# Normalised rows turned by VectorE in 32x32 blocks and placed by a trip through DRAM, for the first six token tiles of LN1

## The chip, the cores and the metric

The kernel runs on one core of one Trainium2 chip. The metric is device time of one execution in microseconds (us). Of three runs of the kernel before, the median is 2017.85 us, the lowest 2013.26, the highest 2018.37. A separate execution was profiled; its trace gives the lines in this document.

The core has five engines with instruction queues of their own: TensorE (PE in the trace, with PEld for its weight loads), VectorE (DVE), ScalarE (ACT), GpSimd (POOL) and SyncE (SP). TensorE multiplies operands from SBUF into PSUM, the accumulator memory. VectorE and ScalarE read SBUF and PSUM. DMA transfers are issued here from the queues of SP and ACT.

## The reference

One layer of a bidirectional encoder, 1024 tokens by 1024 features, float32. Cut to what matters here:

```python
h = layer_norm(x, ln_in_g, ln_in_b)
proj = h @ w_in                                  # attention and recurrence inputs, gates
...
merged = sigmoid(ga) * (att @ w_att_up) + sigmoid(gh) * (rec @ w_hgrn_up)
h = layer_norm(alpha * h + merged @ w_o, ln1_g, ln1_b)
gate, up = split(h @ w_ffn_in)                   # 1024 x 5632
h = layer_norm(alpha * h + (silu(gate) * up) @ w_ffn_out, ln2_g, ln2_b)
```

`layer_norm` takes the mean and variance over the 1024 features of a token, normalises, and applies a gain and a shift per feature. The change lies between the first LN1 (the fifth line) and the product with `w_ffn_in`: the normalised rows have tokens on partitions, and the FFN product needs features on partitions.

## The kernel before

**Stages.** The kernel runs three phases one after the other on the same engines: LN of the input, the projection, attention and recurrence (phase 1); the two up-projections, the gates, W_o and LN1 (phase 2); the FFN and LN2 (phase 3). Each large product is split into three: a float32 operand is cast to a short form "hi" (ScalarE) and a remainder "lo" (GpSimd or VectorE, line 229), and `mm3` (lines 277 to 279) adds hi x hi, hi x lo and lo x hi. The FFN products go by a scheme of Winograd and Strassen kind: seven products of half size (`PRODUCTS`) on sums and differences of the operand's quarters. The quarters and sums of LN1's result are called b11, b21, b22, t1, t2, t3 and t4, and are kept as pairs in `self.xb`.

**The stage of the change** is the last loop of `phase2` (lines 1532 to 1577), over eight tiles `t` of 128 tokens. For each tile:

- `split` makes the hi and lo of the merged activations (`mh`, `ml`).
- `y` (two buffers) is loaded from `ahs_d` by SP: alpha times the residual (line 1545).
- `half(0)` and `half(1)` each multiply by one half of W_o: 24 matmuls of 128x512 into one of four PSUM banks ("pj"), which line 1554 adds to `y` on VectorE.
- `rest(t, y)` takes statistics (lines 206 to 215), normalises (`normalise`, line 300 on ScalarE; for tile 7 half of it on VectorE, line 1524), calls `h1_blocks`, and stores the normalised rows to `n1_d` from ACT's queue (line 1530).

`h1_blocks` turns the 128x1024 rows with `transposed` (lines 302 to 308): two groups of four TensorE transposes by the identity, each into a PSUM bank ("sd"). From the bank, gain and shift are applied per feature (line 1600 on ScalarE, line 1602 on VectorE). Tiles 0 to 3 give b11 and b21, and `w11` (line 1609). Tiles 4 to 7 give t1 (line 1626), b22, t2, t3 and t4; t1 and t2 are put in place at once, the others are stored to `td` in DRAM (line 1618) and read back by `ffn_again` (line 1737).

The order for tiles 0 and 1 is half(0) of both, half(1) of tile 0, `rest(0)`, half(1) of tile 1. After tile 7's halves the first two products (on b11 and b21) of the first three FFN column groups are written ahead of `rest(7)`.

**What sets the order.** The program is given to a planner that simulates all engines with estimated costs, and issues what is ready by priority, which is the order of the program; `high_priority` moves instructions ahead in that order. The result is a fixed list per engine and queue. On the chip each list runs in order, and an instruction that waits holds up those behind it in its list.

**Buffers.** Pool `ws` has a tag "wkeep" with three buffers of 128x512. In the FFN, `keep` (line 1680) copies partial products into them, the first three in the products written ahead of `rest(7)`. Before that the tag isn't used in this stage. A buffer is free when every reader of its tile is done.

Of the kernel before, what the change touches and what calls it, by code (L numbers as in the profile page):

```python
# [10 lines left out]
F32 = mybir.dt.float32  # L11
# [11 lines left out]
HALF = 512  # L23
# [56 lines left out]
class Block:  # L80
    evac_ahead = 1000

    def __init__(self, ctx, tc, x, ln_in_g, ln_in_b, w_in, hgrn_lb, hgrn_norm_g, w_att_up, w_hgrn_up,
                 w_o, ln1_g, ln1_b, w_ffn_in, w_ffn_out, ln2_g, ln2_b, tabs, out, dbg=None):
        self.tc, self.nc, self.ctx = tc, tc.nc, ctx
        self.x = x[0]
        self.ln = {"in": (ln_in_g, ln_in_b), "1": (ln1_g[0], ln1_b[0]), "2": (ln2_g[0], ln2_b[0])}
        self.w_in, self.lbw, self.ng = w_in[0], hgrn_lb, hgrn_norm_g[0]
        self.wa, self.wr, self.wo = w_att_up[0], w_hgrn_up[0], w_o[0]
        self.wfi, self.wfo, self.tabs, self.out = w_ffn_in[0], w_ffn_out[0], tabs, out[0]  # L90
        self.dbg = dbg or {}
        nc = self.nc

        self.npj = 0
        self.issued = {}
        self.psum = ctx.enter_context(tc.tile_pool(name="psum", bufs=1, space=PSUM))
        self.cst = ctx.enter_context(tc.tile_pool(name="cst", bufs=1))
        self.tiny = ctx.enter_context(tc.tile_pool(name="tiny", bufs=1))
        self.spare = self.pad(self.cst, CST_PAD)
        self.wpool = self.pool("wp", "right")  # L100
        self.wp = self.wpool.__enter__()
        dram = ctx.enter_context(tc.tile_pool(name="dram", bufs=1, space=DRAM))

        def scratch(name, n):
            if name in self.dbg:
                return [self.dbg[name][i] for i in range(n)]
            return [dram.tile([128, 1024], F32, name=f"{name}{i}") for i in range(n)]

        self.att_d = scratch("att", 4)
        self.rec_d = scratch("rec", 8)  # L110
        self.tg_d = scratch("tg", 16)
        self.n1_d = scratch("n1", 8)
        self.ahs_d = scratch("ahs", 8)
        self.hg_d = [{n: dram.tile([128, T], F32, name=f"hg{h}{n}") for n in ("t0", "t1", "q")}
                     for h in range(8)]
        self.at_d = [{(k, g): dram.tile([128, T], F32, name=f"at{j}{k}{g}") for k in "qk" for g in range(3)}
                     for j in range(4)]
        for h in range(8):
            self.hg_d[h].update({n: dram.tile([T, 128], F32, name=f"hg{h}{n}") for n in "vg"})
        for j in range(4):  # L120
            self.at_d[j].update({("v", g): dram.tile([T, 128], F32, name=f"at{j}v{g}") for g in range(3)})
        self.w_d = [dram.tile([32, 128], F32, name=f"wd{j}") for j in range(4)]
        self.td = [dram.tile([128, 4, HALF], F32, name=f"td{i}") for i in range(3)]
        self.gd = {p: dram.tile([128, NF // 2, HALF], F32, name=f"gd{p}") for p in range(1, 8)}
        self.consts()
# [1289 lines left out]
    def phase2(self):  # L1415
        nc = self.nc
        with ExitStack() as es:
# [27 lines left out]
            for d in range(8):  # L1445
                t = tgate(d)
# [27 lines left out]
            for d in range(8):  # L1474
                t = tgate(8 + d)
# [23 lines left out]
            for z in (rows, self.recp, self.stp):  # L1499
# [4 lines left out]
                       for n in ("t1", "b11", "b21", "t2")}  # L1504
            yp = es.enter_context(self.pool("yp"))
            w11 = [(yp if k < 3 else self.ws).tile([128, HALF], F32, name="w11", tag=f"w11{k}" if k < 3 else "wsum",
                                                   bufs=1 if k < 3 else 3) for k in range(4)]
            raws = []

            def follow():  # L1510
# [5 lines left out]
                self.again = {n: self.ffn_again(n, 384) for n in ("b22", "t3")}  # L1516
                self.spread("b22")

            def rest(t, y):

                with self.tc.high_priority(offset=2 * self.evac_ahead if t == 7 else 0):
                    mv = self.stats(yp, y, "1")
                    if t == 7:
                        nc.vector.tensor_scalar(y[:, 0:HALF], y[:, 0:HALF], mv[:, 0:1], mv[:, 2:3], op0=OP.subtract,
                                                op1=OP.mult)
                        self.normalise(yp, y[:, HALF:D], y[:, HALF:D], mv)
                    else:
                        self.normalise(yp, y, y, mv)
                    self.h1_blocks(yp, t, y, w11, last=t >= 3)
                nc.scalar.dma_start(self.n1_d[t], y)  # L1530

            for t in range(8):
                ms = []
                for k0 in (0, 4):
                    mh, ml = self.granules()
                    tk = slice(128 * (t % 4), 128 * (t % 4) + 128)
                    if t < 4:
                        for k in (0, 2):
                            self.split(mh[:, k:k + 2, :], ml[:, k:k + 2, :], m0[(k0 + k) // 2][:, :, tk],
                                       eng_lo="dve" if t == 0 and k0 else "pool")  # L1540
                    else:
                        self.split(mh, ml, m1[:, k0:k0 + 4, tk])
                    ms += [(mh[:, k, :], ml[:, k, :]) for k in range(4)]
                y = yp.tile([128, D], F32, name="y1", tag="y1", bufs=2)
                nc.sync.dma_start(y, self.ahs_d[t])

                def half(hh, y=y, ms=ms, t=t):
                    ps = self.ps_pj()
                    for k, (mh, ml) in enumerate(ms):
                        whi, wlo = (z[:, k, :] for z in wo[hh])  # L1550
                        self.mm3(ps, mh, ml, whi, wlo, k == 0, k == KT - 1)
                    s = slice(HALF * hh, HALF * (hh + 1))
                    with self.tc.high_priority(offset=self.evac_ahead if t == 7 else 0):
                        nc.vector.scalar_tensor_tensor(y[:, s], ps, 0.5, y[:, s], op0=OP.mult, op1=OP.add)

                half(0)
                if t == 0:
                    second = half, y
                    continue
                if t == 1:  # L1560
                    second[0](1)
                    rest(0, second[1])
                half(1)
                if t == 7:
                    follow()
                if t in (5, 6):
                    raws.append(self.ffn_raws(t - 5))
                if t == 6:
                    raws.append(self.ffn_raws(2, self.wraw, ("wraw0", "wraw1"), 1))
                if t == 7:  # L1570
                    self.first_groups = [self.wino_project(raws[f], lambda *a, f=f: self.first_evac[f](*a), 1 + f)
                                         for f in range(3)]
                    for g in self.first_groups:
                        next(g)
                rest(t, y)
                if t == 7:
                    self.spread("t3", self.t2_last)
# [2 lines left out]
    PRODUCTS = {5: ("s1", "t1"), 1: ("a11", "b11"), 2: ("a12", "b21"), 6: ("s2", "t2"), 3: ("s4", "b22"),  # L1580
                7: ("s3", "t3"), 4: ("a22", "t4")}

    def h1_blocks(self, pool, t, y, w11, last=False):

        nc = self.nc
        c = slice(128 * (t % 4), 128 * (t % 4) + 128)
        gc, bc = self.col["g1"], self.col["b1"]

        def put(name, v):
            hi, lo = self.xb[name]  # L1590
            return self.split(hi[:, :, c], lo[:, :, c], v,
                              eng_lo="dve" if last else "pool")

        def scaled(q, ps, on_act):

            v = pool.tile([128, 4, 128], F32, name="tsv", tag="tsv", bufs=2)
            for k in range(4):
                g, b = (z[:, 4 * q + k:4 * q + k + 1] for z in (gc, bc))
                if k in on_act:
                    nc.scalar.activation(v[:, k, :], ps[k], AF.Identity, bias=b, scale=g)  # L1600
                else:
                    nc.vector.tensor_scalar(v[:, k, :], ps[k], g, b, op0=OP.mult, op1=OP.add)
            return v

        if t < 4:
            ps = self.transposed(y, 0)
            v = scaled(0, ps, ())
            for k in range(4):
                nc.scalar.activation(w11[k][:, c], ps[k], AF.Copy, scale=gc[:, k:k + 1])
            put("b11", v)  # L1610
            put("b21", scaled(1, self.transposed(y, 1), (0, 2)))
            return

        def later(i, name, v):
# [6 lines left out]
            return pool.tile([128, 4, 128], F32, name="tsum", tag="tsum", bufs=3)  # L1621

        t1, t2 = tmp(), tmp()
        ps = self.transposed(y, 0)
        for k in range(4):
            ins = nc.vector.scalar_tensor_tensor(t1[:, k, :], ps[k], gc[:, k:k + 1], w11[k][:, c], op0=OP.mult,
                                                 op1=OP.subtract)
        b22 = scaled(1, self.transposed(y, 1), (0, 1, 2, 3) if t < 7 else (0, 2))
        put("t1", t1)
        nc.vector.tensor_sub(t2, b22, t1)  # L1630
        self.t2_last = put("t2", t2).ins.name
# [440 lines left out]
```

## Time and profile before

| | |
|---|---|
| median of three runs | 2017.85 us |
| the profiled execution's own time | 2016.71 us |
| its span, first to last instruction | 2014.9 us |
| granted TensorE clock (mean) | 0.997 |
| the stage's W_o matmuls | 1279.64 to 1372.93 us in the span |
| transposes of `h1_blocks` (line 306) | 64, from 1304.8 to 1385.4 us |

All other times in this document are us from the start of the span, unless ns is written. In rows of instructions, `out<-in` names the tiles written and read (buffer numbers left out), `xN` counts instructions, and a bracket at the end holds the idle time ahead of an instruction and what ended it. Matmuls overlap, so the distance between their starts, not their duration, is what each one costs. In rows of windows, the numbers are busy us of the engines, with counts. In rows of DMA issues, the last number is the median time in us from issue to landing.

### The profile page before, as it was taken

Reading aid. Unit: us, or ns where it says so; the run is one execution under the profiler, and the core shown is the slowest. Engines: PE = TensorE matmul, PEld = TensorE weight load, DVE = VectorE, ACT = ScalarE, POOL = GpSimd, SP = SyncE. Lnnn points to the kernel's source line nnn. Section 1 sums busy time; section 2 is a strip of 40 time slices with the busy share of each in tenths; the row PEclk is TensorE's granted clock in tenths of the full one; section 3 lists DMA queues with packets and bytes.
Section 4 is the critical chain, followed back from the end, with each engine's and each line's share of the span. In section 5 each row is a group of like instructions: output and inputs, shape, how many; then the busy total and the mean of one; then the engine's idle time right before and its main releaser. Section 6 shows DMA issues by size and latency. Waiting matters only on the chain. (4 is left out here: it accounts for less than half of the span.)

```text
span 2014.9 us, 30820 instructions
## 1 busy us (share of the span) xinstructions
PE 1980.5 (98%) x10718; PEld 1640.8 (81%) x10718; DVE 1364.5 (68%) x2217; ACT 907.1 (45%) x1822; POOL 1006.3 (50%) x874
## 2 busy tenths in 40 slices
PE   7999999999999999999999999999999999999998
PEld 6688888888888888888888888888788888888886
DVE  7877746885467855797443236558777776767788
ACT  6554455543654446444464443345333333344541
POOL 6466643666455654565546562244666665620000
PEclk9999999999999999999999999999999999999999
DMA  5445645546455464555546377534434443447533
GB/s 162 126 121 151 164 131 149 140 119 173 108 158 141 132 156 118 152 147 151 141 122 190 121 252 245 156 121 141 140 127 136 145 137 125 144 166 276 167 103 123
DMA packets 416125, 301.17 MB, mean 149 GB/s; under 512 B 133153, under 2 KB 359394, under 8 KB 415970
## 3 DMA queue, kind: packets, MB, share of 16 engines
q1 hardware_dynamic: 410624, 282.14, 47.9%
q10 hardware_dynamic: 5346, 17.08, 2.2%
q8 instruction: 84, 1.38, 0.3%
q14 instruction: 71, 0.58, 0.1%
HBM read 204.96 MB, written 94.18 MB: 148 GB/s over the span
## 5 line engine op out<-in xcount | busy, mean ns | idle before, releaser
L229 POOL TENSOR_TENSOR w_lo<-wa,w_hi 128x512 fp32r<-128x512 f32 x272 | 366.3, 1355 | 230.5 <-ACT w_hi L219 216.6
L219 ACT CAST w_hi<-wa 128x512 fp32r<-128x512 f32 x272 | 168.2, 620 | 263.7 <-PE pj L278 166.2
L229 POOL TENSOR_TENSOR w_lo<-wsum,w_hi 128x512 fp32r<-128x512 f32 x88 | 127.8, 1462 | 111.1 <-PE sd L279 60.7
L229 POOL TENSOR_TENSOR w_lo<-f_raw,w_hi 128x512 fp32r<-128x512 f32 x66 | 101.2, 1540 | 51.5 <-ACT w_hi L219 50.3
L215 POOL TENSOR_TENSOR mv<-mv,mhalf 128x1 f32<-128x1 f32 x16 | 12.6, 790 | 221.7 <-DVE mv L214 221.6
L219 ACT CAST w_hi<-wsum 128x512 fp32r<-128x512 f32 x88 | 54.6, 621 | 116.7 <-PE sd L278 108.8
L277 PE MATMUL pj<-xt1hi,w_hi 128*128 128x512 f32 x252 | 99.0, 393 | 0.7 <-DVE evh L589 0.7
L219 ACT CAST gwsum<-a_raw 128x512 fp32r<-128x512 f32 (+1 forms) x78 | 48.1, 617 | 112.2 <-PE pj L278 56.0
L278 PE MATMUL pj<-xt1lo,w_hi 128*128 128x512 f32 x252 | 98.5, 391 | 0.0
L279 PE MATMUL pj<-xt1hi,w_lo 128*128 128x512 f32 x252 | 98.2, 390 | 0.0
L607 DVE TENSOR_TENSOR evh<-wkeep,pj 128x512 f32<-128x512 f32 x45 | 30.8, 685 | 99.4 <-PE pj L279 58.1
L727 POOL TENSOR_TENSOR wa<-wa,wa 128x512 f32<-128x512 f32 x46 | 65.8, 1431 | 57.1 <-DVE wa L726 56.2
L229 POOL TENSOR_TENSOR w_lo<-ws,w_hi 128x512 fp32r<-128x512 f32 x46 | 62.9, 1374 | 56.3 <-ACT w_hi L219 45.8
L755 ACT COPY wkeep<-pj 128x512 f32<-128x512 f32 x136 | 79.4, 585 | 4.9 <-DVE evh L577 4.7
L277 PE MATMUL pj<-xt2hi,w_hi 128*128 128x512 f32 x192 | 77.2, 403 | 2.0 <-ACT w_hi L219 2.0
L279 PE MATMUL pj<-xt2hi,w_lo 128*128 128x512 f32 x192 | 76.3, 397 | 2.0 <-POOL w_lo L229 2.0
L229 DVE TENSOR_TENSOR gwkeep<-a_raw,gwsum 128x512 fp32r<-128x512 f32 (+1 forms) x78 | 53.1, 681 | 36.1 <-ACT gwsum L219 33.3
L278 PE MATMUL pj<-xt2lo,w_hi 128*128 128x512 f32 x192 | 76.1, 396 | 0.8 <-DVE xt2lo L409 0.7
L277 PE MATMUL pj<-xt4hi,w_hi 128*128 128x512 f32 x192 | 76.2, 397 | 0.0
L278 PE MATMUL pj<-xb11lo,w_hi 128*128 128x512 f32 x192 | 75.3, 393 | 0.0
L278 PE MATMUL pj<-xt4lo,w_hi 128*128 128x512 f32 x192 | 75.2, 392 | 0.0
L277 PE MATMUL pj<-xb11hi,w_hi 128*128 128x512 f32 x192 | 75.0, 393 | 0.1
(438 smaller groups left out, 6481.7 us busy)
## 6 DMA issues: line engine op xcount, KB each, us to landing
wa<-in_w_in_dram SPq DMA_DIRECT2D x184, 256.0 KB, 3.4
f_raw<-in_w_ffn_in_dram SPq DMA_DIRECT2D x44, 512.0 KB, 4.2
a_raw<-gd SPq DMA_DIRECT2D x30, 512.0 KB, 3.6
gd<-fc SPq DMA_DIRECT2D x44, 256.0 KB, 2.0
gd<-fs SPq DMA_DIRECT2D x33, 256.0 KB, 2.5
tg<-evh SPq DMA_DIRECT2D x32, 256.0 KB, 3.4
tg<-tg SPq DMA_DIRECT2D x16, 512.0 KB, 5.9
y<-ahs SPq DMA_DIRECT2D x16, 512.0 KB, 6.6
```

What stands on the lines that cost most here:

```text
L215: nc.gpsimd.tensor_tensor(mv[:, 2:3], mv[:, 2:3], self.mhalf[:, 0:1], OP.pow)
L219: ins = nc.scalar.copy(hi, src) if eng_hi == "act" else nc.vector.tensor_copy(hi, src)
L229: ins = e.tensor_sub(lo, src, hi.bitcast(F32))
L277: nc.tensor.matmul(ps, whi, xhi, start=first, stop=False, **kw)
L278: nc.tensor.matmul(ps, whi, xlo, start=False, stop=False, **kw)
L279: self.product = nc.tensor.matmul(ps, wlo, xhi, start=False, stop=last, **kw).ins.name
L607: self.left(nc.vector.tensor_add(t, add, ps))
L727: nc.gpsimd.tensor_sub(a["a21"], a["a22"], a["a11"])
L755: nc.scalar.copy(t, ps)
```

## The change

For tiles 0 to 5, the TensorE transposes are replaced. A new function `h1_turn` runs in `rest`, after normalise. For each half of the 1024 features:

1. VectorE transposes the 128x512 half in 32x32 blocks (sixty-four blocks, each turned in its place) into a buffer `turn`.
2. SP stores the buffer to a DRAM tile `h1_d[t][q]` (256 KB, 128 rows of 2 KB).
3. Four loads on SP, one for each group of 32 partitions, read it back into a buffer `turned`, with the blocks in the order that makes a full transpose: 64 KB each, in pieces of 128 bytes, 512 pieces a load.

Both buffers come from the tag "wkeep" (three buffers; one token tile takes four). `h1_blocks` then reads `turned` in SBUF instead of the PSUM bank. Its call is put off: `rest` appends it to a list, and the list is run after `half(1)` of the next tile, ahead of that tile's `rest`. For tile 0 that is half(1) of tile 1, for tile 5 it is half(1) of tile 6. Tiles 6 and 7 keep the TensorE transposes and the old place. The store to `n1_d` stays where it was.

```diff
+        self.h1_d = [[dram.tile([128, HALF], F32, name=f"h1{t}{q}") for q in range(2)] for t in range(6)]
...
+            turns = []
+
             def rest(t, y):
...
                         self.normalise(yp, y, y, mv)
-                    self.h1_blocks(yp, t, y, w11, last=t >= 3)
+                    if t < 6:
+                        z = self.h1_turn(t, y)
+                        turns.append(lambda: self.h1_blocks(yp, t, z, w11, last=t >= 3))
+                    else:
+                        self.h1_blocks(yp, t, y, w11, last=t >= 3)
                 nc.scalar.dma_start(self.n1_d[t], y)
...
                     rest(0, second[1])
                 half(1)
+                while turns:
+                    turns.pop(0)()
                 if t == 7:
                     follow()
...
+    def h1_turn(self, t, y):
+        nc, out = self.nc, []
+        for q in range(2):
+            a = self.ws.tile([128, HALF], F32, name="turn", tag="wkeep", bufs=3)
+            nc.vector.transpose(a, y[:, HALF * q:HALF * (q + 1)])
+            nc.sync.dma_start(self.h1_d[t][q], a)
+            o = self.ws.tile([128, HALF], F32, name="turned", tag="wkeep", bufs=3)
+            z = self.h1_d[t][q].rearrange("(a i) (k b j) -> b i k a j", a=4, b=4, j=32)
+            for b in range(4):
+                nc.sync.dma_start(o[32 * b:32 * b + 32, :].rearrange("i (k a j) -> i k a j", a=4, j=32), z[b])
+            out.append([o[:, 128 * k:128 * (k + 1)] for k in range(4)])
+        return out
+
     def h1_blocks(self, pool, t, y, w11, last=False):
...
+        turned = y if type(y) is list else None
+
+        def features(q):
+            return turned[q] if turned else self.transposed(y, q)
...
         if t < 4:
-            ps = self.transposed(y, 0)
+            ps = features(0)
             v = scaled(0, ps, ())
...
-            put("b21", scaled(1, self.transposed(y, 1), (0, 2)))
+            put("b21", scaled(1, features(1), (0, 2)))
             return
...
-        ps = self.transposed(y, 0)
+        ps = features(0)
         for k in range(4):
             ins = nc.vector.scalar_tensor_tensor(t1[:, k, :], ps[k], gc[:, k:k + 1], w11[k][:, c], op0=OP.mult,
                                                  op1=OP.subtract)
-        b22 = scaled(1, self.transposed(y, 1), (0, 1, 2, 3) if t < 7 else (0, 2))
+        b22 = scaled(1, features(1), (0, 1, 2, 3) if t < 7 else (0, 2))
```

## The prediction

> **What bounds the kernel now.** The first view is the page: shares of busy time by engine over the whole span. TensorE (PE) is busy 98% of it, VectorE (DVE) 68%.
>
> ```profile
> span 2014.9 us, 30820 instructions
> PE 1980.5 (98%) x10718; PEld 1640.8 (81%) x10718; DVE 1364.5 (68%) x2217; ACT 907.1 (45%) x1822; POOL 1006.3 (50%) x874
> ```
>
> An average over the span doesn't tell what this stage is worth, so the second view is busy time by window for the stage of W_o and LN1. The columns are the window, the busy time of PE, PEld, DVE, ACT and POOL, the granted clock, the DMA share and GB/s.
>
> ```profile
> 1326.40:1338.00 11.60, 11.60 (x57) 9.71 (x56) 6.43 (x14) 5.30 (x12) 5.64 (x5) 1.00 0.25 93
> 1349.50:1360.40 10.90, 10.90 (x50) 9.04 (x49) 7.29 (x16) 3.80 (x7) 3.60 (x3) 1.00 0.50 164
> 1360.40:1372.90 12.50, 12.50 (x65) 10.54 (x64) 9.41 (x24) 6.11 (x13) 3.12 (x3) 1.00 0.47 148
> 1372.90:1390.20 17.30, 17.30 (x82) 14.35 (x81) 14.23 (x26) 11.36 (x21) 8.28 (x7) 1.00 0.53 167
> 1390.20:1400.00 9.80, 8.96 (x40) 7.14 (x39) 9.76 (x17) 3.53 (x7) 3.13 (x3) 1.00 0.10 28
> ```
>
> PE has no gap up to 1390, at full clock. DVE is half idle in the early tiles (6.43 of 11.60) and nearly full at the end (14.23 of 17.30, then 9.76 of 9.80). So TensorE work taken out of this stage is worth its full length as long as nothing else is late. At the end DVE decides whether that stays so.
>
> **What is removed.** The third view is PE's timeline round the first group of transposes (start, us busy, line, out<-in).
>
> ```profile
> 1279.64 0.39 PE L277 MATMUL pj<-wo0hi,w_hi 128*128 128x512 f32 x1
> ...
> 1290.52 0.39 PE L277 MATMUL pj<-wo1hi,w_hi 128*128 128x512 f32 x1
> ...
> 1304.57 0.39 PE L279 MATMUL pj<-wo0hi,w_lo 128*128 128x512 f32 x1
> 1304.80 1.03 PE L306 MATMUL sd<-tabs_sb,y 128*128 128x128 f32 x8
> 1305.59 0.48 PE L277 MATMUL pj<-wo0hi,w_hi 128*128 128x512 f32 x1
> 1305.91 0.40 PE L278 MATMUL pj<-wo0lo,w_hi 128*128 128x512 f32 x1
> ...
> 1372.93 0.39 PE L277 MATMUL sd<-xb11hi,w_hi 128*128 128x512 f32 x1
> ```
>
> The durations overlap, so I go by starts. The 48 matmuls from 1279.64 to 1290.52 take 10.88 us, 0.227 us each. Without the eight transposes L278 would start 2 x 0.227 after 1304.57, at 1305.03; it starts at 1305.91. A group of eight therefore costs 0.88 us, not its 1.03 us of busy time. Cross-check over the stage: up to the first product of the FFN (the last row shown) it holds 384 matmuls and the seven groups of tiles 0 to 6, so 384 x 0.227 + 7 x 0.88 = 93.3 us, and 1372.93 - 1279.64 is 93.29. The change removes six groups: **6 x 0.88 = 5.3 us off PE**. Tiles 6 and 7 keep theirs. This is the whole gross gain, 0.26% of the time.
>
> **What is added and moved.** Per tile: two DVE block turns, two 256 KB stores, and eight loads of 64 KB, cut into 512 pieces of 128 B each. The nearest rows are the kernel's other block turns, their scattered stores in pieces of the same size, and a td store (first the instruction rows with min/median/max ns, then the time to landing; in the second fence number, size and us to landing).
>
> ```profile
> L589 DVE STREAM_TRANSPOSE evh<-evh x30: 645/700/715, 82.8 to 960.4; 128x512 f32<-128x512 f32 x30
> L598 SPq DMA_DIRECT2D at3v<-evh x24: 313/498/526, 908.1 to 971.7; - x24
> DMA to landing us min/median/max: 1.8/2.0/7.0
> ```
>
> ```profile
> td<-tsum SPq DMA_DIRECT2D x7, 256.0 KB, 2.6
> ```
>
> DVE: 12 x 0.70 = 8.4 us. The ten turns of tiles 0 to 4 lie in DVE's idle half (6.43 of 11.60 busy) and cost nothing; without that cover they would cost their 7.0 us. Tile 5's 1.4 us fall towards the full end. The reads of the four features now come from SBUF instead of PSUM. Bounds for one 128x128: 0.40 us (DVE from PSUM) and 0.34 us (DVE, all in SBUF, though another operation):
>
> ```profile
> L1602 DVE TENSOR_SCALAR tsv<-sd,vc x26: 398/403/413, 1305.4 to 1389.4; 128x128 f32<-128x128 f32 x26
> L1635 DVE SCALAR_TENSOR_TENSOR tsum<-tsum,vc,w x16: 335/344/1186, 1352.0 to 1392.9; 128x128 f32<-128x128 f32 x16
> ```
>
> I take no difference; a tile has four to six of them on DVE, at most 0.4 us either way.
>
> SP queue: per tile 8 x 0.50 + 2 x 0.35 (estimated, as the shorter issues of L598) = 4.7 us of issuing, in a tile of 10.9 us. Behind the waiting loads stand the y load of the tile after next, the td stores of tiles 4 to 6 and the t_raw reloads. The y load has four PSUM banks, two tiles or 22 us, of cover; the reloads of b22 and t3 feed products from 1402.20 on (row in the part on tile 7). These I cost at nothing; with the cover gone each would cost about one landing, 5.1 us for a y load.
>
> ```profile
> y<-ahs SPq DMA_DIRECT2D x8, 512.0 KB, 5.1
> ```
>
> **The trip** from the end of normalise: first turn 0.7, store 2.6, four loads issued in 2.0, landing 2.0 after the last: 7.3 us for the first half, 9.3 for the second, four issues later. A scattered *load* is nowhere in this trace. A packet's price is bounded by two windows of queue q1: one with almost only 128 B stores (60.3% x 4.1 us x 16 engines / 2256 = 17.5 ns) and one of 512 B weight reads (49.5% x 4.5 x 16 / 1125 = 31.7 ns).
>
> ```profile
> q1 hardware_dynamic: 2256, 0.52, 60.3%
> ...
> q1 hardware_dynamic: 1125, 0.57, 49.5%
> ```
>
> A tile's 4096 packets take 4.5 to 8.1 us of all 16 engines, on top of the 0.25 to 0.50 that they are busy already: between 0.7 and over 1 of a 10.9 us tile. I take the lower end, since size and shape are those of the stores, and keep the other for the range.
>
> **Where the gain can leak** is tile 7, so the last view is DVE, ACT and PE round it.
>
> ```profile
> 1356.37 1.25 ACT L300 ACTIVATE y<-y,mv 128x1024 f32<-128x1024 f32 x1 [4.83 <-DVE mv L299]
> 1362.49 1.12 DVE L1626 SCALAR_TENSOR_TENSOR tsum<-sd,vc,w 128x128 f32<-128x128 f32 x4 [0.18 <-PE sd L306]
> 1371.09 1.12 DVE L1626 SCALAR_TENSOR_TENSOR tsum<-sd,vc,w 128x128 f32<-128x128 f32 x4 [1.27 <-PE sd L306]
> 1381.87 1.50 DVE L1524 TENSOR_SCALAR y<-y,mv 128x512 f32<-128x512 f32 x1 [0.45 <-POOL mv L215]
> 1384.50 0.60 PE L306 MATMUL sd<-tabs_sb,y 128*128 128x128 f32 x4
> 1388.72 0.78 DVE L229 TENSOR_TENSOR xt1lo<-tsum,xt1hi 128x512 fp32r<-128x512 f32 x1 [0.37 <-ACT xt1hi L219]
> 1390.18 0.39 PE L277 MATMUL sd<-xt1hi,w_hi 128*128 128x512 f32 x1
> ...
> 1399.80 0.50 PE L279 MATMUL pj<-xt2hi,w_lo 128*128 128x512 f32 x1 [0.84 <-POOL w_lo L229]
> ...
> 1402.20 0.39 PE L277 MATMUL sd<-xb,w_hi 128*128 128x512 f32 x1
> ```
>
> The same stretch as one window, columns as above:
>
> ```profile
> 1360.46:1389.50 29.04, 29.04 (x142) 24.25 (x140) 22.98 (x49) 16.71 (x32) 10.84 (x9) 1.00 0.52 163
> ```
>
> Read in order: tile 5 is normalised by 1357.62, DVE builds its blocks from 1362.49, tile 6's from 1371.09, and from there has almost no gap until it normalises tile 7 at 1381.87. That leaves 1.1 us until PE's transposes of tile 7 and, further on, 0.7 us (1389.50 to 1390.18) until the first product that reads t1. To keep all 5.3 us, DVE must run this whole chain 5.3 us earlier. From 1360.46 to 1389.50 it has 29.04 - 22.98 = 6.1 us idle. The window shrinks by tile 5's group, 0.9, and up to 1.4 us of turns come in, so 3.8 us of idle time remain: enough in sum. But tile 5's blocks now hang on the trip. With five groups gone (4.4 us) it is normalised by 1353.2 and its halves are there at 1360.5 and 1362.5. To be 5.3 us early the blocks would have to start at 1357.2. They are 3.3 us late, and 1.3 us of that goes into the gap before 1371.09. **About 2 us are given back.** Bounds: 0 (the planner moves stats of tile 6 into the wait) and 5.3 (all of it).
>
> Sum, against the profiled execution (span 2014.9, 2016.71 with what lies around it): 2016.7 - 5.3 + 2.0 = 2013.4, 3.3 us less. Of three runs the median, 2017.85, stands 1.1 above it: 2014.5 on that scale.
>
> **The rivals.** *All of it stays*, 5.3 us: 2012.5. For it: PE has no idle time to 1390, and DVE's idle time exceeds its new work. Against it: the trip of 7.3 to 9.3 us against the 4.9 between normalise and blocks in tile 5 now.
>
> *No change*: the end of DVE's chain doesn't move, because the trip is as late as PE is early; PE then waits about 5 us before tile 7's transposes: 2017.9. For it: slack of 1.1 and 0.7 us there. The Trainium skill (VectorE: DVE Perf Modes, "Rules for kernel authors") speaks for this: it gives 128x128 transposes to TensorE wherever a PSUM destination will do, as it does here. By that rule the work goes to the engine that the windows above show full at the end; they agree there, and not for the earlier tiles.
>
> *Slower*: the three-slot ring ("wkeep") that holds four tiles per token tile. A load can start only when the blocks of the tile before have read their half. One round is 2.0 of issue, a landing of 2.0 to 7.0 (the slowest scattered store), 3.2 to read both halves (8 x 0.40), and up to 2 us behind the next tile's evacuation and statistics: 7.2 to 14.2 us. It decides from 10.9 us up, a tile's time on PE. At 14.2, 3.3 us are lost on each of five rounds, 16.5; less 3.8 of DVE idle time and the 5.3 gained, 7.4 are left: 2025.3. For it: over 1 of DMA at the upper packet price. Against it: the landing median of 2.0. The Trainium skill (DMA: Bandwidth & Descriptors, Specifications) puts line rate at 512 B and more per transfer; the pieces here are 128 B, and no run so far shows such a load.
>
> That the change doesn't do what it says can hardly be: no TensorE instruction is left for tiles 0 to 5.
>
> **Chances.** The forecast 0.37, all of it stays 0.19, no change 0.20, slower 0.24. A measurement of this kernel can tell about 0.3%, 6 us, from no change: below 2011.8 is faster, above 2023.9 slower. The gross gain lies under that bound, so faster needs something besides: the gap of 0.84 before 1399.80 and others in the products after it, whose order the planner makes anew, and a low run (the three spread over 5 us). I give 0.17: most of the all-stays case's upper half and a little of the forecast. Slower gets 0.25, nearly all of the ring's case and a little of no change. Same is 0.58. The range goes down to 2009 (5.3 kept and 3.5 of scatter and later gaps) and up to 2027, past the ring's case by some of the runs' spread. The likeliest case's own range is 2012.5 to 2018.
>
> **What would show it.** Right: 16 transposes on L306 instead of 64; the two halves' matmuls following at 0.227 us without gaps; tile 7's last W_o matmul 5.3 us earlier relative to the stage's start; DVE's first block instruction of tile 5 waiting on a DMA; a gap on PE of about 2 us before tile 7's transposes or the first xt1 product. Wrong: a PE gap in tiles 1 to 6 (the ring, seen as DVE turns or SP loads waiting on DVE or ACT reads of "turned"), scattered loads landing after 5 us or more, DMA share near 1 through the stage, or an order of the later FFN products with other gaps than before, which this sum leaves out.

## The result and the profile after

The changed kernel takes 2027.53 us (median of four runs, 2027.41 to 2028.87), against 2015.59 for the kernel before in the same comparison (four runs, 2013.26 to 2018.37). The ratio is 1.0062, with a 95% interval of 1.0047 to 1.0078: **slower by 0.6%**, half a microsecond above the top of the range predicted. The profiled execution took 2028.87 us, with a span of 2027.1.

For every kernel below I use one stage measure, S: from the first W_o matmul to the first product that reads xt1. Before it was 1390.18 - 1279.64 = 110.5 us. With six groups of transposes gone and nothing else late it would be 110.5 - 5.3 = 105.2. Lines of code move by one to seven in the changed kernels (L306 is L307, L277 is L278 and so on; the block lines shift most). TensorE's timeline of the changed kernel (start, us busy, line, out<-in, idle before and what ended it):

```profile
1275.62 0.39 PE L278 MATMUL pj<-wo0hi,w_hi 128*128 128x512 f32 x1
...
1371.78 1.97 PE L307 MATMUL sd<-tabs_sb,y 128*128 128x128 f32 x8 [8.39 <-ACT y L301]
1373.40 0.78 PE L278 MATMUL sd<-xb11hi,w_hi 128*128 128x512 f32 x1
...
1377.91 0.39 PE L278 MATMUL sd<-xb21hi,w_hi 128*128 128x512 f32 x1
...
1399.46 0.80 PE L278 MATMUL sd<-xt1hi,w_hi 128*128 128x512 f32 x1 [6.83 <-ACT xt1hi L220]
```

S is 1399.46 - 1275.62 = 123.8, which is 13.3 longer than before and 18.6 longer than 105.2. Two gaps make 15.2 of the 18.6: 8.39 ahead of tile 6's transposes and 6.83 ahead of the first xt1 product. Some 2.5 more is matmuls at a lower speed behind the 8.39 gap: the transposes take 1.62 instead of 0.88, and the next twelve matmuls 4.51 (1373.40 to 1377.91) instead of 12 x 0.227 = 2.72.

Who is late at the 8.39 gap can be followed back. PE waited for ACT's normalise of tile 6. The rows of DVE and ACT, then those of SP's queue (a SP row is issuing, not transfer):

```profile
1359.08 2.18 DVE L1653 SCALAR_TENSOR_TENSOR tsum<-turned,vc,w 128x128 f32<-128x128 f32 x4 [2.05 <-DMA turned<-h]
...
1364.87 1.29 DVE L1561 SCALAR_TENSOR_TENSOR y<-pj,y 128x512 f32<-128x512 f32 x2 [2.23 <-DMA y<-ahs]
```

```profile
1366.16 1.65 ACT L1627 ACTIVATE tsv<-turned,vc 128x128 f32<-128x128 f32 x4 [3.73 <-DMA turned<-h]
...
1370.48 1.24 ACT L301 ACTIVATE y<-y,mv 128x1024 f32<-128x1024 f32 x1 [1.23 <-DMA td<-tsv]
```

```profile
1338.82 0.57 SPq L1597 DMA_DIRECT2D h<-turn  x1
1342.71 2.60 SPq L1601 DMA_DIRECT2D turned<-h  x4
1345.41 0.57 SPq L1597 DMA_DIRECT2D h<-turn  x1
1346.02 0.43 SPq L1552 DMA_DIRECT2D y<-ahs  x1
1347.99 2.96 SPq L1601 DMA_DIRECT2D turned<-h  x4
1351.06 1.48 SPq L1597 DMA_DIRECT2D h<-turn  x1
1354.54 2.60 SPq L1601 DMA_DIRECT2D turned<-h  x4
1357.24 0.57 SPq L1597 DMA_DIRECT2D h<-turn  x1
1357.85 0.43 SPq L1552 DMA_DIRECT2D y<-ahs  x1
...
1371.40 0.46 SPq L1552 DMA_DIRECT2D y<-ahs  x1
```

SP goes store, wait, four loads, store, y load, wait, four loads for every tile. From tile 3's first store (1338.82) to tile 4's (1351.06) it needs 12.2 us, and 10.8 to 13.2 from tile to tile between tiles 1 and 5, while PE without transposes needs 48 x 0.227 = 10.9. So the y loads slip. There is a second reason. A y load writes over the buffer of the tile two before it, which that tile's second block turn still reads; the turns of tiles 3 to 5 end at 1343.45, 1355.69 and 1367.96, and the y loads follow 2.2 to 3.4 us behind, which is the part of SP's list. The last of them is issued 95.8 us after the stage began (1371.40 - 1275.62); before, it was 83.3 (1362.96 - 1279.64):

```profile
1362.96 0.32 SPq L1545 DMA_DIRECT2D y<-ahs  x1
```

VectorE then evacuates both halves of tile 6 only at 1364.87, behind the wait for y, and behind its reads of tile 4's `turned` half at 1359.08. This y load took 6.9 us to land, the longest of the eight. VectorE's last step for the normalise, after the statistics, ran from 1370.30 to 1370.45; the store to `td` that the normalise's bracket names is what came last by the profile. In the changed kernel's waits over the stage (engine, line, what it waited for: us in total, times, longest), first all engines, then SP's queue:

```profile
ACT tsv L1627 <- DMA turned<-h: 21.7, 6, 5.3
DVE tsv L1629 <- DMA turned<-h: 20.7, 4, 11.0
...
DVE y L1561 <- DMA y<-ahs: 7.8, 5, 2.2
```

```profile
SPq L1601 <- DMA h<-turn: 25.1, 12, 3.3
```

The trip's size, from its DMA issues (number, KB each, median us to landing):

```profile
h<-turn SPq DMA_DIRECT2D x12, 256.0 KB, 2.5
turned<-h SPq DMA_DIRECT2D x48, 64.0 KB, 3.3
```

The stage's excess over the time before is 13.3, and the time behind the stage is 627.6 instead of 624.7, mostly matmuls at the lower speed behind the second gap. That is 16.2; the two profiled times differ by 12.2, since the changed kernel's profile had reached this stage 4.0 us earlier. Over all profiles of this study the stage began anywhere from 1274.7 to 1281.6, the order of the work ahead of it being untouched by the change. I use S for that reason; it comes from one execution of each kernel, so how far S varies from run to run is not known, and the timed ratios stand beside it where there are any. One execution of 5115.2 us, of the kernel with four tiles and the reads held, is left out of its ratio; its cause is not known.

### The profile page after: what moved, and what is told of

It reads as the page before. It is cut to its first block, busy times and chain, and to the rows that moved or that the text cites. A ratio compares the mean times of both kernels' runs of the same rounds, so it can differ in the third digit from the quotient of the medians.

```text
span 2027.1 us, 30849 instructions
## 1 busy us (share of the span) xinstructions
PE 1978.2 (98%) x10670; PEld 1636.3 (81%) x10670; DVE 1365.1 (67%) x2229; ACT 908.3 (45%) x1822; POOL 1010.1 (50%) x874
## 5 line engine op out<-in xcount | busy, mean ns | idle before, releaser
L230 POOL TENSOR_TENSOR w_lo<-wsum,w_hi 128x512 fp32r<-128x512 f32 x88 | 132.7, 1518 | 111.1 <-PE sd L280 60.7
L278 PE MATMUL pj<-xt1hi,w_hi 128*128 128x512 f32 x252 | 98.9, 392 | 0.7 <-DVE evh L590 0.7
L278 PE MATMUL pj<-xt2hi,w_hi 128*128 128x512 f32 x192 | 77.1, 403 | 2.0 <-ACT w_hi L220 2.0
L278 PE MATMUL pj<-xt4hi,w_hi 128*128 128x512 f32 x192 | 76.1, 396 | 0.0
L278 PE MATMUL pj<-xb11hi,w_hi 128*128 128x512 f32 x192 | 74.8, 392 | 0.2 <-ACT w_hi L220 0.2
```

Of the source, the lines that this page charges most:

```text
L230: ins = e.tensor_sub(lo, src, hi.bitcast(F32))
L278: nc.tensor.matmul(ps, whi, xhi, start=first, stop=False, **kw)
```

## The experiments

Each kernel is the changed one with the edit shown.

| kernel | S, us | time ratio to before (95%) |
|---|---|---|
| before | 110.5 | 1 |
| changed | 123.8 | 1.0062 (1.0047 to 1.0078) |
| blocks put off, TensorE's transposes kept | 110.5 | 0.9999 (0.9989 to 1.0009) |
| trip made, not read | 124.3 | one run, 2029.84 us |
| the same, y loads from ACT's queue | 115.9 | one run, 2021.78 us |
| f_raw loads later | 121.1 | one run, 2026.50 us |
| plain loads, blocks not placed | 112.4 | one run, 2020.32 us |
| wide buffers | 116.3 | 1.0043 (1.0030 to 1.0056) |
| tiles 4 and 5 alone | 117.0 | one run, 2023.99 us |
| tiles 0 to 3 alone | 114.2 | 1.0025 (1.0013 to 1.0038) |
| tiles 0 to 3, wide | 111.0 | 1.0001 (0.9989 to 1.0013) |
| tiles 0 to 3, wide, two tiles later | 111.0 | 1.0003 (0.9990 to 1.0017) |
| tiles 0 to 4, wide, two tiles later | 111.0 | 1.0016 (1.0004 to 1.0027) |
| tiles 0 to 3, wide, reads held | 112.7 | 1.0023 (1.0012 to 1.0034) |
| tiles 0 to 3, wide, reads held, f_raw later | 110.8 | 1.0016 (1.0004 to 1.0027) |
| six tiles, wide, reads held | 111.8 | 1.0015 (1.0003 to 1.0026) |

The kernel before had medians of 2013 to 2015 us beside these.

### Is it the putting off, or the trip?

Blocks one tile later, from TensorE's transposes at the old place:

```diff
-                        z = self.h1_turn(t, y)
+                        z = [self.transposed(y, q) for q in range(2)]
```

> Edit: TensorE transposes stay for all tiles, at the old place; only the building of the blocks of tiles 0 to 5 is put off behind half(1) of the next tile, reading the PSUM banks. If putting it off by itself hurts (blocks of tile 5 late on VectorE behind the statistics): S 112 to 116, with a gap before tile 7's transposes. If it is harmless, as all theories of the trip have it: S 109.5 to 111.5, time within 0.3% of before.

S 110.5, ratio 0.9999, no gap on PE. Putting the blocks off costs nothing.

The trip made but not read, with the blocks from the transposes at the old place (the turned halves go unused):

```diff
                     if t < 6:
-                        z = self.h1_turn(t, y)
-                        turns.append(lambda: self.h1_blocks(yp, t, z, w11, last=t >= 3))
-                    else:
-                        self.h1_blocks(yp, t, y, w11, last=t >= 3)
+                        self.h1_turn(t, y)
+                    self.h1_blocks(yp, t, y, w11, last=t >= 3)
```

> Edit: the trip is made for tiles 0 to 5 and its result is read by nothing; the blocks are built from TensorE transposes at the old place, as before the change. It costs what the trip takes from SP, VectorE and the DMA engines, without anything that waits for it. Theory that lateness comes from waiting for the trip (ring, start): S within 2 us of the 110.5 before. Theory that the SP queue or the DMA engines are overloaded by themselves (y loads late behind waits for stores): y loads still issue 4 us or more late, TensorE gaps of 4 us or more, S over 114.

S 124.3: nobody waits for the data, and the stage is as long as in the changed kernel. Its waits, on DVE and on SP:

```profile
DVE y L1559 <- DMA y<-ahs: 17.6, 6, 7.8
DVE turn L1594 <- DMA turned<-h: 9.4, 3, 5.8
```

```profile
SPq L1599 <- DMA h<-turn: 24.1, 12, 4.5
```

VectorE waits for `y`, which stands on SP's list behind 24.1 us of waits for the trip's stores, and for a free slot of the ring before it can turn. The same kernel with the y loads on another queue:

```diff
-                nc.sync.dma_start(y, self.ahs_d[t])
+                nc.scalar.dma_start(y, self.ahs_d[t])
```

> As the kernel that makes the trip for six tiles and does not read it (blocks from TensorE's transposes at the old place; S 124.3, VectorE waiting 17.6 us for y loads), but the y loads are issued from ACT's queue instead of SP's. Theory: the y loads were late because they stood on SP's list behind waits for the trip's stores and buffers; off that list the waits for y fall below 5 us and S comes to 110.5 to 114. Rival: the DMA engines are full (4096 packets of 128 B a tile), and y arrives late from any queue: waits for y 10 us or more, S 118 to 125.

S falls from 124.3 to 115.9, with 110.5 as the mark, since the transposes are kept. The y loads' place behind the trip is thus worth about 8 us. It is not all: the waits for y fell only to 13.8 us, more than the 5 of my theory. What is left of them comes from y's buffer, as DVE's and ACT's rows show: the last y load goes 0.04 us after the second turn of tile 5 has read the buffer, and that turn had waited for a slot of the ring. The three y loads before it follow a turn as closely (0.03 to 0.04 us).

```profile
1367.99 0.71 DVE L1594 STREAM_TRANSPOSE turn<-y 128x512 f32<-128x512 f32 x1 [2.97 <-DMA turned<-h]
1368.74 0.34 ACTq L1550 DMA_DIRECT2D y<-ahs  x1
```

Against full DMA engines as the cause stands that a y load got no slower: 5.1 us to landing before (the prediction's row), 4.7 in the kernel with the unread trip, 4.5 from ACT's queue (medians).

```profile
y<-ahs SPq DMA_DIRECT2D x8, 512.0 KB, 4.7
```

### What makes the trip long?

The f_raw weight loads moved out of the first trip, behind tile 3's:

```diff
-                    raws.append(self.ffn_raws(t - 5))
+                    raws.append(self.ffn_raws(t - 5, after=self.trip[3]))
```

> Edit: the changed kernel with the FFN weight loads (f_raw) of the first three groups put behind the trip of tile 3 on SP; the ring stays. Start theory: the first trip takes 10 us instead of 15, the gaps of 8.4 and 6.8 us shrink to under 4 us in all, S 107 to 112. Ring theory: the first trip is 4 to 5 us earlier, but rounds stay at about 12 us a tile, so that 1.3 us a tile is lost over five tiles; gaps of 8 to 13 us in all, S 114 to 120.

S 121.1, 2.7 less. The longest wait of all, the 11.0 us of DVE in the table of waits, is the one of the first trip; taking the loads out of it mends a small part of the loss at most (one profile of each). The run is not clean: the loads now stand on SP's list ahead of and between the loads of tile 4's halves (4.16 us of issuing from 1344.37 on), so it does not give the price of the first trip alone.

The four scattered loads replaced by one plain 256 KB load of the half (the blocks are not placed: this leaves out half of the transpose):

```diff
-            for b in range(4):
-                nc.sync.dma_start(o[32 * b:32 * b + 32, :].rearrange(...), z[b])
+            nc.sync.dma_start(o, self.h1_d[t][q])
```

> Edit: all six tiles; the four scattered loads of 64 KB are replaced by one plain load of 256 KB in rows of 2 KB. It leaves out the placing of the blocks, so that the values are not turned across blocks; every other instruction and wait is the same. Theory of the scattered load (8 issues of 0.65 us a tile on SP, 4096 packets of 128 B): SP is freed of 4 us a tile, rounds come to 8 to 9 us, the gaps go to 0 to 3 us, S 105.5 to 109. Theory of the round trip (two stores a tile whose landing SP and then VectorE wait for in order): S stays over 115.

S 112.4, so 11.4 of the 13.3 us go with the scattered form: eight issues of 0.65 us a tile become two, and a load lands in 2.9 us for 256 KB instead of 3.3 for 64:

```profile
turned<-h SPq DMA_DIRECT2D x12, 256.0 KB, 2.9
```

The Trainium skill (DMA: Bandwidth & Descriptors, Specifications) puts line rate at 512 B and more; four times the bytes in less time without 128 B pieces agrees with it. Even so a round trip is left: PE had a gap of 3.54 us, and S is 7.2 above 105.2.

The turned halves in two 128x1024 buffers of their own, so that "wkeep" holds only the `turn` halves:

```diff
+        wide = self.wraw.tile([128, D], F32, name="turned", tag=f"wraw{t % 2}", bufs=1)
...
-            o = self.ws.tile([128, HALF], F32, name="turned", tag="wkeep", bufs=3)
+            o = wide[:, HALF * q:HALF * (q + 1)]
```

> Edit: the two turned halves of a tile go into one wide buffer (two such buffers, alternating, that the W_o weights left free); the three slots of wkeep hold the turn buffers alone. S is the time from the first W_o matmul to the first product that reads t1: 110.5 us before, 123.8 after, with gaps on TensorE of 8.4 and 6.8 us. Ring theory (three slots for four tiles make a round of 12.2 us a tile against 10.9 on TensorE, and put each store behind the loads of the other half): both stores go out together, a round falls under 10.9, the gaps go to under 3 us in all, S is 106 to 110. Start theory (four weight loads of 512 KB beside the first trip make it some 8 us late, and nothing is made up afterwards): that burst is still there, gaps of 8 us or more, S over 115. Load theory (eight loads of 64 KB take 0.65 us each on SP and land after 3.3): the issue of 5.2 us a tile stays, but fits into 10.9, S 108 to 112.

S 116.3, 7.5 less. SP now writes both stores first, the y load next, and then all eight loads:

```profile
1348.67 0.92 SPq L1598 DMA_DIRECT2D h<-turn  x2
1350.17 0.32 SPq L1552 DMA_DIRECT2D y<-ahs  x1
1350.85 5.33 SPq L1602 DMA_DIRECT2D turned<-h  x8
```

In the changed kernel the second turn of a tile had to wait until the second half of the tile before was read, as DVE's rows show:

```profile
1336.58 0.70 DVE L1596 STREAM_TRANSPOSE turn<-y 128x512 f32<-128x512 f32 x1
1342.15 0.60 DVE L1629 TENSOR_SCALAR tsv<-turned,vc 128x128 f32<-128x128 f32 x2 [2.27 <-DMA turned<-h]
1342.79 0.66 DVE L1596 STREAM_TRANSPOSE turn<-y 128x512 f32<-128x512 f32 x1
```

That is the three-slot ring at work: the halves of one tile are turned 6.2 us apart, and with them go the stores.

### Where in the stage?

The trip for tiles 0 to 3, and for tiles 4 and 5, alone:

```diff
-                    if t < 6:
+                    if t < 4:
```

> Edit: the trip for tiles 0 to 3 alone; tiles 4 to 7 keep TensorE transposes and the old place. Theory that every tile of the trip adds lateness which TensorE's lead hides until the stage's end, so that only what is still late at tile 7 costs: three to four tiles without a trip let VectorE, half idle, catch up; no gaps over 1 us, S is 110.5 - 4 x 0.88 = 107.0, the time 3 us less than before (ratio 0.998 to 0.999). Theory that a trip costs where it is (SP and DMA busy, TensorE held up in its own tile): two thirds of the loss stay, S over 115, ratio above 1.003.

> Edit: the trip for tiles 4 and 5 alone, so without the burst of weight loads at the start and with two rounds instead of six. Accumulation theory (1.3 us and more of lateness per round from the first trip on): little is late at tile 7, S 108 to 112. Theory of the single trip (12 us from the turn to the last landing, against about 5 between normalise and blocks before, at a place where VectorE has no idle time to make it up): tile 5's own trip is late whatever came before, gaps of 4 us or more, S 113 to 120.

Tiles 0 to 3: S 114.2 where 107.0 was my theory. The loss isn't something that adds up towards the end. PE's fixed order meets the first transposes that are left, those of tile 4, 2.98 us early. Tiles 4 and 5 alone: S 117.0, with a gap of 4.39 us before tile 7's transposes. Either part costs more than it saves; the second is what the theory of the single late trip expected. Four tiles with wide buffers:

> Edit: the trip for tiles 0 to 3 alone as in the run of that kind, and the turned halves in the wide buffers, so that both stores of a tile go out together. By the theory that only lateness at the end costs: the same S as with the narrow buffers, 107.0, and the same time within 0.1%. If lateness from tile 3 still reaches the end with the narrow ring, this one is 1 to 3 us faster than the other.

S 111.0, ratio 1.0001: no change. Here one thing was left, which ACT's rows show:

```profile
1345.10 1.28 ACT L1637 ACTIVATE w<-turned,vc 128x128 f32<-128x128 f32 x4 [5.13 <-DMA turned<-h]
...
1347.02 1.24 ACT L301 ACTIVATE y<-y,mv 128x1024 f32<-128x1024 f32 x1
```

Tile 4's normalise stood behind reads of tile 3's turned half, whose trip was still on its way.

### The reads' place in the order

Two tiles later instead of one, for tiles 0 to 3 and for 0 to 4:

```diff
-                while turns:
-                    turns.pop(0)()
+                while turns and turns[0][0] <= t - 2:
+                    turns.pop(0)[1]()
```

> As the first-four-tiles kernel with wide buffers, but the blocks of tile t are built after half(1) of tile t+2 instead of t+1. S is the stage measure of the other experiments, first W_o matmul to first product reading xt1 (110.5 us before; 111.0 with blocks one tile later, where tile 4's normalise on ACT stood behind w11 reads of tile 3 that waited 5.1 us for the trip). Theory: what costs is only that DVE and ACT stand in order behind reads of a trip that takes longer than one tile; with two tiles of cover no read waits more than 1 us, no gap on PE before tile 4's transposes, S = 110.5 - 4 x 0.88 = 107.0, ratio about 0.9983. Rival, SP's list: y loads stay late behind the store waits, the W_o evacuations wait for them and a gap of 2 us or more stays at tile 4: S 109 to 111, ratio 1.000.

> The same with tile 4 on the trip as well (tiles 0 to 4, blocks two tiles later). Theory (only the reads' waits cost): tile 4's blocks come before tile 6's statistics, its trip ends some 10 us earlier, S = 110.5 - 5 x 0.88 = 106.1. Rival: the td stores of tile 4 and their read-back come later and SP is busy with f_raw loads there, so tile 7's chain is late: S 108 to 112, a gap of 2 us or more before tile 6's or 7's transposes or the first xt1 product.

S 111.0 for both, where 107.0 and 106.1 were expected. With five tiles the W_o part is 4.1 us shorter (89.2), and the loss comes behind it, as the rival had it: a gap of 2.14 us before tile 7's transposes, with slow matmuls after it. With four tiles the run didn't test what it was made for. The planner issues what it believes is ready, and put the reads where they had been; ACT still waited 4.83 us ahead of the same normalise:

```profile
1345.97 1.28 ACT L1637 ACTIVATE w<-turned,vc 128x128 f32<-128x128 f32 x4 [4.83 <-DMA turned<-h]
1347.16 1.22 ACT L301 ACTIVATE y<-y,mv 128x1024 f32<-128x1024 f32 x1
```

So the order was forced: every read of tile t's turned halves goes behind tile t+1's normalise.

```diff
+                ins = nc.scalar.activation(w11[k][:, c], ps[k], AF.Copy, scale=gc[:, k:k + 1])
+                if turned:
+                    self.behind(ins, self.norm_last)
```

(and likewise for the other reads, with the blocks called after `rest` of the next tile)

> First four tiles on the trip, wide buffers, and every read of a turned half of tile t is ordered behind the normalise of tile t+1 on ACT. S as before (before 110.5, same kernel without that order 111.0). Theory: the loss is reads that the order puts ahead of the next tile's normalise while the trip is still on its way; with them behind it, tile 4's normalise waits for no turned half, the gap of 2.2 us on PE before tile 4's transposes goes, S = 110.5 - 4 x 0.88 = 107.0 and the ratio 0.998 to 0.999. Rival: y loads late on SP's list (one waited for 7.0 us) hold the evacuations instead: S 109 to 112.

> The same, and the f_raw loads of the first three FFN groups placed behind the trip of tile 3 instead of in the first trip. Theory: with the reads already held back, the burst of loads costs nothing or at most 1 us: S 106.5 to 107.5. Rival (the burst makes the trips and y loads late): S lower than without it by 2 us or more.

> All six tiles on the trip, wide buffers, reads of tile t's turned halves ordered behind the normalise of tile t+1 (without that order S 116.3, after 123.8, before 110.5). If the order of reads was the whole loss: S = 110.5 - 6 x 0.88 = 105.2. If the trips of tiles 4 and 5 are also too long for the place where they are needed (their t1, t2 and the td stores come before tile 7's chain): gaps before tile 7's transposes and the first xt1 product, S 110 to 114. If neither: S stays 116.

In the first, the gap before tile 4 is gone, and the stage's W_o part lasts 89.8 us instead of 93.3: all of 4 x 0.88 saved. Yet S is 112.7 and not 107.0, with 3.69 us of idle time at the first xt1 product. The f_raw loads moved away give 110.8, 1.9 less (one profile of each), where 106.5 to 107.5 were expected; its W_o part is longer again, 91.9 us, with a gap of 1.92 us. With all six tiles S is 111.8, 4.5 less than without the order, and PE's rows and two windows show where the saving went:

```profile
1276.45 0.39 PE L278 MATMUL pj<-wo0hi,w_hi 128*128 128x512 f32 x1
...
1365.73 0.39 PE L278 MATMUL sd<-xb11hi,w_hi 128*128 128x512 f32 x1
...
1383.36 0.39 PE L280 MATMUL pj<-xb21hi,w_lo 128*128 128x512 f32 x1
1388.28 1.22 PE L278 MATMUL sd<-xt1hi,w_hi 128*128 128x512 f32 x2 [4.53 <-ACT xt1hi L220]
```

The W_o part ends 89.3 us after its start (1276.45 to 1365.73), 4.0 us sooner than before. Products on b11 and b21 go on to 1383.36; then PE waits 4.53 us. The last 19.2 us before the first xt1 product, as windows (columns as in the prediction), of this kernel and then of the kernel before:

```profile
1369.00:1388.20 19.20, 14.58 (x67) 11.31 (x65) 19.08 (x35) 10.34 (x20) 10.48 (x7) 0.99 0.53 164
```

```profile
1371.00:1390.20 19.20, 19.20 (x93) 16.00 (x92) 15.36 (x30) 12.73 (x24) 8.60 (x8) 1.00 0.50 155
```

VectorE is busy 19.08 of 19.20 us, against 15.36 before. It is the bound at the end, and TensorE's saving becomes a wait for it. Not all of this is added work: some instructions ran far longer than their kind (one of L1669 1385 ns, with a median of 339), in this window and in that of before; why, no run here shows. With four tiles another engine was late there. The first xt1 product waited for ACT's cast of xt1, whose input VectorE had ready at 1382.49; on ACT's list it stood behind the casts of values read back from `td` and other work, and the first of those casts waited (ACT's rows in the four-tile kernel with reads held):

```profile
1383.91 0.83 ACT L220 CAST xt<-t_raw 128x768 fp32r<-128x768 f32 x1 [2.25 <-DMA t_raw<-td]
...
1386.73 0.61 ACT L220 CAST xt1hi<-tsum 128x512 fp32r<-128x512 f32 x1
```

The way the end of the chain binds differs from kernel to kernel; that it didn't come earlier is common to all. No version tried beat the kernel before.

## Why the prediction was wrong

**The gross gain** of 6 x 0.88 = 5.3 us was right. With six tiles and the reads held, the W_o part is 4.0 us shorter, and its one gap, of 1.09 us at tile 6's transposes, is most of the rest.

**"These I cost at nothing"** (SP's issues, and what stands behind the waiting loads) is the step that failed first. I counted SP's issuing, 4.7 us a tile, and took the four PSUM banks as 22 us of cover for the y load. But SP's list is in order, and each half's loads wait for its store to land: 25.1 us of waits in twelve halves, 2.1 each. In the tile shown above, from 1338.82 on, the list holds waits of 3.3 and 1.5, loads of 2.6 and 3.0, and 1.6 for the stores and the y load: 12.0 of its 12.2 us, above the 10.9 of PE. An issue was 0.65, not 0.50. The four rounds from tile 1's first store to tile 5's took 48.0 us (1314.90 to 1362.87) against 4 x 10.9, so a tile eats about 1 us of the cover. Nor are the four banks the whole cover: y has two buffers, and the block turns, which the ring delays, hold them longer, so a y load can't start early. An evacuation that is late holds statistics and normalise behind it. The unread trip shows that the trip's queue and buffers alone, with no block waiting for the data, make 13.8 us of loss (124.3 over the 110.5 of a stage with all its transposes).

**"The trip"** of 7.3 and 9.3 us from the end of normalise was mis-sized. Tile 3's second half was read on ACT 15.0 us after the tile's first store was issued (1338.82 to 1353.84):

```profile
1353.84 0.88 ACT L1627 ACTIVATE tsv<-turned,vc 128x128 f32<-128x128 f32 x2 [3.12 <-DMA turned<-h]
```

My sum had 8.6 for the same stretch (9.3 less the turn). The landing was 3.3 instead of 2.0, the issue 2.6 instead of 2.0, the store's landing let the loads start 3.9 us after its issue instead of 2.6, and the second half's loads did not follow 2.0 us later ("four issues later") but 5.3 (1342.71 to 1347.99), behind the ring and a store of their own. A smaller term was put at nothing as well ("I take no difference"): the eight t1 reads of `turned` took 608 ns in the mean, up to 1418, against 340 for the eight that still read PSUM. That is about 1 us a tile, where I had 0.4 at most; in the kernel with wide buffers they took 344 to 352, so it isn't the main loss.

**"About 2 us are given back"**, at tile 7, took the loss at one place only. It came at two, 8.39 us at tile 6's transposes and 6.83 at the first xt1 product. The bound of 5.3 there was no bound, since nothing in it could make PE later than before.

**The rivals.** The slower one was nearest. Its mechanism (a round of the three-slot ring longer than a tile's time on PE) happened, with a round of 12.2 inside its 7.2 to 14.2 and past its point of 10.9; wide buffers took back 7.5 of 13.3 us. Its price, 2025.3, was low though the round was shorter than priced: I had not seen that the wait also sits on SP's list ahead of the y loads. *No change* describes what was left once ring and order were mended: PE early and waiting 4.53 us for DVE's chain, at the first xt1 product and not at tile 7's transposes. By the rule of the Trainium skill (VectorE: DVE Perf Modes, "Rules for kernel authors"), the transposes stay on TensorE; the 19.08 of 19.20 us on VectorE agree.

**What would show it**: the PE gap and the late reads on DVE were named, and the first gap came at a tile I had named under the ring. The slow landing, named as 5 us or more, was 3.3 in the median and 6.2 at most. The DMA share was 0.72 and 0.69 in the windows round the first gap (rows at the end), not near 1.

What stays open is why the four timed runs of the changed kernel lost 12 us and not the 16 that stage and tail add up to; one profile can't tell whether all four began the stage early.

## What to carry to other kernels

A transpose by way of DRAM costs its queue more than its issues: the load's wait for the store stands in an in-order list, and all that is listed behind it waits too. Before moving a few microseconds off the bound engine, sum a tile's waits and issues on the queue that takes them, and compare that with the tile's time on the bound engine. Ask which buffers the new reads hold longer, and what load is waiting to fill them. Look, too, where the reads of such a trip stand on the in-order engines: ahead of work that could go on, each of their waits is passed on.

## What was not expected of the hardware

A gap of some microseconds on TensorE can cost more than its length. After the 8.39 us gap the matmuls start 0.43 us apart instead of 0.227, for some 5 us. The same follows shorter gaps; the shortest with it in W_o's part is one of 1.89 us, in the kernel with four tiles and blocks two tiles later:

```profile
1348.44 1.63 PE L307 MATMUL sd<-tabs_sb,y 128*128 128x128 f32 x8 [1.89 <-ACT y L301]
...
1350.72 0.63 PE L278 MATMUL pj<-wo0hi,w_hi 128*128 128x512 f32 x1
1351.15 0.63 PE L279 MATMUL pj<-wo0lo,w_hi 128*128 128x512 f32 x1
...
1352.35 0.40 PE L279 MATMUL pj<-wo0lo,w_hi 128*128 128x512 f32 x1
```

There the lower speed lasts to about 1352.3, 3.9 us. The gap's length alone does not decide: in the kernel with four tiles, reads held and f_raw later, a gap of 1.92 us was followed by transposes at the full speed and matmuls 0.23 us apart.

```profile
1359.41 1.09 PE L307 MATMUL sd<-tabs_sb,y 128*128 128x128 f32 x8 [1.92 <-ACT y L301]
```

The slow matmuls are how a kernel whose gap (1.89 or 2.19 us) is shorter than the saving of four groups (3.5) still ends with no gain: S 111.0 is 107.0, the gap, and some 2 us of slow matmuls.

The granted clock says the same: 0.78 and 0.84 in the two windows round the first gap of the changed kernel, where it was 1.00 before it.

```profile
1360.40:1371.80 11.40, 3.01 (x15) 2.16 (x13) 8.95 (x20) 4.72 (x9) 2.37 (x3) 0.78 0.72 189
1371.80:1388.00 16.20, 16.20 (x67) 13.53 (x68) 11.76 (x24) 8.34 (x18) 5.72 (x5) 0.84 0.69 190
```

The Trainium skill (TensorE: Matmul & The Clock Gate, "HAM oscillation — how this bites in real kernels") gives about 3.4 us as the idle time from which the clock drops. In these traces 1.89 us was enough in one kernel and 1.92 was not in another; the measurement decides.
